# One-hot operations of an expert-gate scatter: per-token rows read from PSUM, two products in one operation

## The chip, the cores and the metric

One core of a Trainium2 chip runs the whole program. The metric is device time in microseconds (us), the median of several executions. One more execution is taken with the hardware profiler, and every row below is from it. Engines: PE is the matrix engine (PEld its weight loads), DVE the vector engine, ACT the scalar engine, POOL the GpSimd engine, and SP issues most DMAs. Each engine runs its own instructions in the order in which they were written, and semaphores make it wait for the others.

## The reference, cut to what matters

The program is one encoder block on 512 tokens of width 1024, in fp32: a convolution branch and windowed attention, both merged into x, and then PEER, a retrieval over 16384 experts that are one neuron each. The part around the change is PEER:

```python
q = (hc @ w_query).reshape(TOKEN_CHUNK, 8, 2, 128)
sc = einsum('thpd,pnd->thpn', q, sub_keys)          # 8 heads, 2 halves, 128 keys
vals, idx = top_k(sc, 16)
cand = vals[:, :, 0, :, None] + vals[:, :, 1, None, :]
top_s, pos = top_k(cand, 16)                        # 16 experts (i*128 + j) per head
gate = softmax(top_s)
act = gelu(einsum('thkd,td->thk', expert_u[expert_idx], hc))
out = einsum('thk,thkd->td', gate * act, expert_v[expert_idx])
```

So each token has 8 x 16 = 128 triples (i, j, gate).

## The kernel before, in words

Tokens are handled in four tiles of 128. For tile 0 the chosen rows of the expert tables are gathered. For tiles 1 to 3 (384 tokens) the whole tables are multiplied: with `hps`, PE computes U·h for each block of 128 experts (a "U block", `u_block`, 24 matmuls in split fp32: `uhi` from ACT, `ulo` from POOL, three products), ACT applies Gelu (`hb`), DVE multiplies by the dense gates (`hb<-hb,gt`), and PE accumulates the product with V in six PSUM tiles (`acc`, a "V block", 18 matmuls). The loop over 128 expert blocks at the end of the program, the V stage, does both. Thirty U blocks, the lead, are done ahead of it and kept in SBUF.

The dense gates G[token, i, j] are made by `build(t)`, once per tile t = 1, 2, 3, between the top-k and the V stage. It transposes i, j and gate to have the 128 triples on the partitions (L584, into `tp`), writes them as fp16 into `tt`, each number twice in a row, so that a row can be read in pairs (L591 by ACT; L592 by DVE; the gate, times 32768, as a high and a low half). Then, for each group of eight tokens (16 groups per tile, 48 in all):

- L607, DVE: `oij` = (0..127 == i) and (0..127 == j) for eight tokens, 2048 fp16 elements per partition;
- L609, DVE, twice: `ohl` = one-hot of j times the high, then the low half of the gate, 1024 elements each;
- L615 and L616, PE: for each token, `gp` = high part and low part times one-hot of i, 16 matmuls;
- L618, ACT: two copies of four tokens each from `gp` (PSUM) to `st`.

After every fourth group (`c`), a DMA on SP (L619) stores `st`, 2 MB, to `gates_dram`. The V stage reads it back as `gt` (L665), so the first V block waits for the last store.

`oij` and `ohl` have two buffers each. Of the eight PSUM banks the U blocks use two, `tp` one and `gp` five.

The order of instructions on an engine is not the order of this text. A scheduler takes the recorded operations, with its own estimate of each one's time, and sets an order per engine: lead U blocks, the top-k of tile 0 (`first_topk`, `select`) and the builds are interleaved by it. Only the loop of the V stage has POOL's order fixed by hand.

Of the kernel before, what the change touches and what calls it, by code (L numbers as in the profile page):

```python
# [7 lines left out]
F32 = mybir.dt.float32  # L8
F32R = mybir.dt.float32r
F16 = mybir.dt.float16  # L10
I32 = mybir.dt.int32
U32 = mybir.dt.uint32
AF = mybir.ActivationFunctionType
OP = mybir.AluOpType
# [3 lines left out]
P = 128  # L18
# [9 lines left out]
NKEY = 128  # L28
# [6 lines left out]
TB8 = 8  # L35
# [9 lines left out]
def encoder_block(ctx, tc, x, g1, w_in, taps, dwb, lng, lnb, w_pw, sink, w_o, w_out, g2, g2row,  # L45
                  w_query, keys, ut, u, v, gfin, out):
    nc = tc.nc
    ACT, DVE, POOL, PE, SP = nc.scalar, nc.vector, nc.gpsimd, nc.tensor, nc.sync
# [68 lines left out]
    with ExitStack() as fc:  # L117
# [15 lines left out]
        with ExitStack() as x0c:  # L133
# [6 lines left out]
            with tc.manual_schedule(engines=ordered):  # L140
                ACT.activation(warm, epst, AF.Sqrt)
                for t in range(NT):
                    a = x0.tile([P, D], F32, name="xt", bufs=NT)
# [32 lines left out]
        with ExitStack() as ac:  # L176
# [45 lines left out]
            for i in range(2):  # L222
                ps = proj(w_in[26 + i], hT)
                a = aw.tile([P, 4, 3 * P], F32, name="L", bufs=3).rearrange("p a b -> p (a b)")[:, :S]
# [176 lines left out]
        for j in range(KD):  # L401
            ps = proj(w_pw[j], acT, lo_engine=DVE)
            a = sg[0][:, j, :]
# [42 lines left out]
    with ExitStack() as rc:  # L446
# [27 lines left out]
        def lead(n):  # L474
            for _ in range(n):
                if nlead[0] < LEAD:
                    u_block(nlead[0])
                    nlead[0] += 1
# [40 lines left out]
        with qc:  # L519
# [44 lines left out]
            for h in range(HP):  # L564
                scs = []
                for p in range(2):
                    n = 2 * h + p
# [11 lines left out]
        psg = rc.enter_context(tc.tile_pool(name="psg", bufs=2, space=PSUM))  # L579

        def build(t):
            tp = psg.tile([P, 3, P], F32, name="tp", bufs=1)
            for s in range(3):
                PE.transpose(tp[:, s, :], ij[t][:, s].rearrange("p h k -> p (h k)"), ident)  # L584
            def twice(s):
                a = tp[:, s, :].rearrange("p (g t) -> p g t", t=TB8)
                return a[..., None].to_broadcast([P, P // TB8, TB8, 2])

            tt = gw.tile([P, P // TB8, 4, TB8, 2], F16, name="tt", bufs=2)
            for s in range(3):  # L590
                ACT.activation(tt[:, :, s], twice(s), AF.Copy, scale=1.0 if s < 2 else GSC)  # L591
            DVE.scalar_tensor_tensor(tt[:, :, 3], twice(2), GSC, tt[:, :, 2], op0=OP.mult, op1=OP.subtract)  # L592
            for c in range(P // GT):
                st = gw.tile([P, NKEY, GT], F32, name="st", bufs=2)
                for q8 in range(GT // TB8):
                    lead(0)
                    n = c * GT + q8 * TB8
                    oij, ohl = (gw.tile([P, 2, TB8, NKEY], F16, name=nm, bufs=2) for nm in ("oij", "ohl"))

                    def rows(s):  # L600
                        a = tt[:, n // TB8, s:s + 2].rearrange("p s t b -> p (s t) b")
                        return a[:, :, None, :].to_broadcast([P, 2 * TB8, NKEY // 2, 2])

                    def prs(a):
                        return a.rearrange("p s t (a b) -> p (s t) a b", b=2)

                    DVE.tensor_tensor(prs(oij), iota8, rows(0), op=OP.is_equal)  # L607
                    for s in range(2):
                        DVE.tensor_tensor(prs(ohl)[:, s * TB8:(s + 1) * TB8], prs(oij)[:, TB8:],  # L609
                                          rows(2)[:, s * TB8:(s + 1) * TB8], op=OP.mult)  # L610
                    for q4 in range(TB8 // 4):
                        gp = psg.tile([P, 4, NKEY], F32, name="gp", bufs=5)
                        for k in range(4):
                            m = q4 * 4 + k
                            PE.matmul(gp[:, k, :], ohl[:, 0, m, :], oij[:, 0, m, :], start=True, stop=False)  # L615
                            PE.matmul(gp[:, k, :], ohl[:, 1, m, :], oij[:, 0, m, :], start=False, stop=True)  # L616
                        o = q8 * TB8 + q4 * 4
                        ACT.activation(st[:, :, o:o + 4], gp.rearrange("p t i -> p i t"), AF.Copy, scale=1.0 / GSC)  # L618
                SP.dma_start(gdram[:, :, (t - 1) * (P // GT) + c].rearrange("g j i t -> j g i t"),  # L619
                             st.rearrange("p (g i) t -> p g i t", i=GI))  # L620

        for t in range(1, NT):
            build(t)
# [197 lines left out]
```

## Time and profile before

| what | us |
| --- | --- |
| median of 3 runs (lowest, highest) | 1814.74 (1811.3, 1815.37) |
| the profiled execution's own time | 1812.98 |
| its span | 1811.2 |
| PE busy in it | 1734.4 (96%) |
| DVE busy | 1432.8 (79%) |
| POOL busy | 961.4 (53%) |
| ACT busy | 770.8 (43%) |

The span runs from the first to the last instruction; 1.8 us of the execution's time lie outside it. A busy share is an average over stages: in most of the span PE is busy without a gap, and in the stage of the builds it is not. Matmul records overlap, since they are pipelined, so PE's pace is read from the distance of their starts and not from their durations.

### The profile page before, as it was taken

To read this page: it belongs to the slowest core of one execution; us is meant where nothing else is said; L and a number is where in the kernel's file an instruction comes from. 1 tells how busy PE (TensorE), PEld (TensorE's weight loads), DVE (VectorE), ACT (ScalarE), POOL (GpSimd) and SP (SyncE) were. 2 spreads that over 40 slices of the span, in tenths; PEclk is the share of its full clock that TensorE was granted. 3 is DMA by queue.
4 is the path that set the end of the run, shared out by engine and by line. 5 is a ranking of instruction groups with operands and counts; after the bars stand their busy time and mean duration, and the time that the engine had idled before them with its cause. 6 is when DMAs were issued, how large, how long until landed. Compare 5 with 4: busy or idle time off the path is not lost.

```text
span 1811.2 us, 25192 instructions
## 1 busy us (share of the span) xinstructions
PE 1734.4 (96%) x8873; PEld 1484.2 (82%) x8873; DVE 1432.8 (79%) x2545; ACT 770.8 (43%) x1374; POOL 961.4 (53%) x741
## 2 busy tenths in 40 slices
PE   6999999989999978888999999999999999999998
PEld 5778877658888877767899999999999999999876
DVE  4999856674536999999989987887787777878874
ACT  4233257883343335555443433333333333333243
POOL 4444421020134445445448888778777778778511
PEclk8999999999999989999999999999999999999999
DMA  4223210024243113777878988888888888898972
GB/s 142 87 92 100 98 59 24 24 82 152 81 148 100 56 59 124 233 214 227 290 257 321 333 309 328 311 318 312 313 317 304 323 317 315 295 332 287 343 259 93
DMA packets 148942, 379.42 MB, mean 209 GB/s; under 512 B 11520, under 2 KB 63760, under 8 KB 148816
## 3 DMA queue, kind: packets, MB, share of 16 engines
q1 hardware_dynamic: 110832, 241.20, 38.1%
q0 software_dynamic: 37120, 134.52, 20.8%
q10 hardware_dynamic: 864, 2.10, 0.3%
q8 instruction: 69, 1.13, 0.2%
q14 instruction: 57, 0.47, 0.1%
HBM read 346.84 MB, written 30.93 MB: 209 GB/s over the span
## 4 chain that ended last, share of the span: by engine, by line
PE 68%; DVE 15%; issue 2%; DMA 2%; ACT 1%; POOL 1%; SPq 0%; POOLq 0%; DVEq 0%; ACTq 0%
PE acc L64 8%; PE acc L63 8%; PE acc L65 8%; PE hps L65 7%; PE hps L64 7%; PE hps L63 7%; PE mm L63 5%; PE mm L65 5%; PE mm L64 4%; DVE ohl L609 4%; DVE oij L607 3%; DMA row<-in_v_dram,eidx 1%; PE s L63 1%; PE pt L290 1%; PE s L64 1%
## 5 line engine op out<-in xcount | busy, mean ns | idle before, releaser
L58 POOL TENSOR_TENSOR ulo<-uraw,uhi 128x512 fp32r<-128x512 f32 x256 | 406.1, 1595 | 290.6 <-ACT uhi L57 271.0
L63 PE MATMUL hps<-big,uhi 128*128 128x384 f32 x1024 | 349.3, 341 | 2.2 <-ACT hb L442 2.1
L65 PE MATMUL hps<-big,ulo 128*128 128x384 f32 x1024 | 349.4, 341 | 0.9 <-POOL ulo L58 0.9
L64 PE MATMUL hps<-big,uhi 128*128 128x384 f32 x1024 | 349.0, 341 | 0.0
L64 PE MATMUL acc<-vlo,ph 128*128 128x512 f32 x768 | 300.7, 392 | 1.6 <-DVE vlo L58 1.6
L65 PE MATMUL acc<-vhi,pl 128*128 128x512 f32 x768 | 299.6, 390 | 0.0
L63 PE MATMUL acc<-vhi,ph 128*128 128x512 f32 x768 | 299.1, 391 | 0.4 <-ACT vhi L57 0.4
L58 POOL TENSOR_TENSOR wlo<-wraw,whi 128x512 fp32r<-128x512 f32 x120 | 157.8, 1318 | 203.5 <-ACT whi L57 202.0
L57 ACT ACTIVATE uhi<-uraw 128x512 fp32r<-128x512 f32 x256 | 160.1, 631 | 233.6 <-PE hps L64 140.9
L643 DVE SCALAR_TENSOR_TENSOR row<-row,h2tok 128x1024 f32<-128x1024 f32 x128 | 189.5, 1487 | 66.4 <-DMA row<-in_u_dram,eidx 66.3
L654 DVE SCALAR_TENSOR_TENSOR yacc<-row,dots,yacc 128x1024 f32<-128x1024 f32 x127 | 177.2, 1396 | 69.7 <-DMA row<-in_v_dram,eidx 69.4
L58 DVE TENSOR_TENSOR vlo<-vraw,vhi 128x1024 fp32r<-128x1024 f32 x128 | 188.6, 1474 | 18.9 <-ACT vhi L57 18.9
L636 POOL DMA_INDIRECT row<-in_u_dram,eidx x128 | 183.8, 1436 | 33.2 <-issue 21.1
L63 PEld LDWEIGHTS hps<-big,uhi 128*128 128x128 f32 x1024 | 194.3, 190 | 6.6 <-ACT hb L442 2.5
L64 PEld LDWEIGHTS hps<-big,uhi 128*128 128x128 f32 x1024 | 194.6, 190 | 4.2
L57 ACT ACTIVATE whi<-wraw 128x512 fp32r<-128x512 f32 x152 | 95.3, 631 | 239.2 <-PE mm L64 125.5
L65 PEld LDWEIGHTS hps<-big,ulo 128*128 128x128 f32 x1024 | 194.2, 190 | 2.0 <-POOL ulo L58 1.9
L636 POOL DMA_INDIRECT row<-in_v_dram,eidx x128 | 165.1, 1290 | 48.7 <-DVE yacc L654 21.5
L57 ACT ACTIVATE ph<-hb 128x384 fp32r<-128x384 f32 x128 | 66.8, 523 | 287.4 <-PE acc L64 274.6
L65 PEld LDWEIGHTS acc<-vhi,pl 128*128 128x128 f32 x768 | 144.2, 188 | 30.9 <-DVE pl L58 0.3
L64 PEld LDWEIGHTS acc<-vlo,ph 128*128 128x128 f32 x768 | 144.2, 188 | 30.0 <-DVE vlo L58 3.7
L63 PEld LDWEIGHTS acc<-vhi,ph 128*128 128x128 f32 x768 | 144.1, 188 | 28.4 <-ACT vhi L57 1.0
(221 smaller groups left out, 3211.7 us busy)
## 6 DMA issues: line engine op xcount, KB each, us to landing
uraw<-in_ut_dram SPq DMA_DIRECT2D x128, 512.0 KB
vraw<-in_v_dram SPq DMA_DIRECT2D x128, 512.0 KB
gates_dram<-st SPq DMA_DIRECT2D x12, 2048.0 KB
gt<-gates_dram SPq DMA_DIRECT2D x32, 768.0 KB
wraw<-in_w_in_dram SPq DMA_DIRECT2D x44, 512.0 KB
wraw<-in_w_query_dram SPq DMA_DIRECT2D x16, 512.0 KB
wraw<-in_w_o_dram SPq DMA_DIRECT2D x8, 512.0 KB
oraw<-in_w_out_dram SPq DMA_DIRECT2D x16, 256.0 KB
```

The source lines that it names most:

```text
L57: ACT.activation(hi, src, AF.Copy)
L58: lo_engine.tensor_tensor(lo, src, f(hi), op=OP.subtract)
L63: PE.matmul(ps, wh, mh, start=first and i == 0, stop=False)
L64: PE.matmul(ps, wh, ml, start=False, stop=False)
L65: PE.matmul(ps, wl, mh, start=False, stop=last and i == n - 1)
L290: PE.transpose(pt[:, i, :], L[:, i, j * P:(j + 1) * P], ident)
L607: DVE.tensor_tensor(prs(oij), iota8, rows(0), op=OP.is_equal)
L609: DVE.tensor_tensor(prs(ohl)[:, s * TB8:(s + 1) * TB8], prs(oij)[:, TB8:], rows(2)[:, s * TB8:(s + 1) * TB8], op=OP.mult)
L636: POOL.indirect_dma_start(out=row, out_offset=None, in_=table, in_offset=bass.IndirectOffsetOnAxis(ap=eidx[:, c:c + 1], axis=0))
L643: DVE.scalar_tensor_tensor(row, row, 1.0, h2tok, op0=OP.mult, op1=OP.mult, accum_out=dots[:, c:c + 1])
L654: DVE.scalar_tensor_tensor(yacc, row, dots[:, c:c + 1], yacc, op0=OP.mult, op1=OP.add)
```

## The change

`tt`, the small table of rows, is copied once per tile by ACT into a PSUM tile `tq`, as 512 fp32 words that hold 1024 fp16 numbers. The one-hot operations read their rows from `tq`. The two products of a group become one operation on 2048 elements, whose other operand, the one-hot of j, is read twice by a stride of zero. The transposes now write a buffer of the `gp` ring, which has four banks instead of five; `tq` has the two that this and `tp` leave.

```diff
--- before.py
+++ after.py
@@ -579,7 +579,7 @@
         psg = rc.enter_context(tc.tile_pool(name="psg", bufs=2, space=PSUM))
 
         def build(t):
-            tp = psg.tile([P, 3, P], F32, name="tp", bufs=1)
+            tp = psg.tile([P, 4, P], F32, name="gp", bufs=4)
             for s in range(3):
                 PE.transpose(tp[:, s, :], ij[t][:, s].rearrange("p h k -> p (h k)"), ident)
             def twice(s):
@@ -590,6 +590,9 @@
             for s in range(3):
                 ACT.activation(tt[:, :, s], twice(s), AF.Copy, scale=1.0 if s < 2 else GSC)
             DVE.scalar_tensor_tensor(tt[:, :, 3], twice(2), GSC, tt[:, :, 2], op0=OP.mult, op1=OP.subtract)
+            tq = psg.tile([P, 512], F32, name="tq", bufs=2)
+            ACT.activation(tq, tt.rearrange("p g s t b -> p (g s t b)").bitcast(F32), AF.Copy)
+            tqv = tq.bitcast(F16).rearrange("p (g s t b) -> p g s t b", s=4, t=TB8, b=2)
             for c in range(P // GT):
                 st = gw.tile([P, NKEY, GT], F32, name="st", bufs=2)
                 for q8 in range(GT // TB8):
@@ -598,18 +601,19 @@
                     oij, ohl = (gw.tile([P, 2, TB8, NKEY], F16, name=nm, bufs=2) for nm in ("oij", "ohl"))
 
                     def rows(s):
-                        a = tt[:, n // TB8, s:s + 2].rearrange("p s t b -> p (s t) b")
+                        a = tqv[:, n // TB8, s:s + 2].rearrange("p s t b -> p (s t) b")
                         return a[:, :, None, :].to_broadcast([P, 2 * TB8, NKEY // 2, 2])
 
                     def prs(a):
                         return a.rearrange("p s t (a b) -> p (s t) a b", b=2)
 
                     DVE.tensor_tensor(prs(oij), iota8, rows(0), op=OP.is_equal)
-                    for s in range(2):
-                        DVE.tensor_tensor(prs(ohl)[:, s * TB8:(s + 1) * TB8], prs(oij)[:, TB8:],
-                                          rows(2)[:, s * TB8:(s + 1) * TB8], op=OP.mult)
+                    jj = oij[:, 1].rearrange("p t (a b) -> p t a b", b=2)
+                    DVE.tensor_tensor(ohl.rearrange("p s t (a b) -> p s t a b", b=2),
+                                      jj[:, None].to_broadcast([P, 2, TB8, NKEY // 2, 2]),
+                                      rows(2).rearrange("p (s t) a b -> p s t a b", s=2), op=OP.mult)
                     for q4 in range(TB8 // 4):
-                        gp = psg.tile([P, 4, NKEY], F32, name="gp", bufs=5)
+                        gp = psg.tile([P, 4, NKEY], F32, name="gp", bufs=4)
                         for k in range(4):
                             m = q4 * 4 + k
                             PE.matmul(gp[:, k, :], ohl[:, 0, m, :], oij[:, 0, m, :], start=True, stop=False)
```

The scheduler sets another order. The lines behind the change are numbered 3 or 4 higher: L607 is now L610, L609 is L612, L615 and L616 are L619 and L620.

On DVE, in the middle of the builds, one group and a half before (`vals`, `topv` and `topi` are the top-k of tile 0):

```order
L458 MAX topv_4514<-rep 128x8
L609 TENSOR_TENSOR ohl<-oij,tt 128x1024 x2
L607 TENSOR_TENSOR oij<-iotar,tt 128x2048
L459 MAX_INDEX topi_4518<-topv_4514,rep 128x8
L609 TENSOR_TENSOR ohl<-oij,tt 128x1024 x2
```

and with the change:

```order
L612 TENSOR_TENSOR ohl<-oij,tq 128x2048
L610 TENSOR_TENSOR oij<-iotar,tq 128x2048
L454 MAX topv_4514<-cand 128x8
L612 TENSOR_TENSOR ohl<-oij,tq 128x2048
L610 TENSOR_TENSOR oij<-iotar,tq 128x2048
```

Two products have become one of twice the size, and the one top-k instruction per group stays behind `oij`. From the first `oij` to the last `ohl`, 57 instructions of DVE that are neither stand before, and 96 with the change: more of tile 0's top-k lies inside the builds.

On PE, where a group's gate matmuls begin (`hps` are lead U blocks), before:

```order
L64 MATMUL hps<-big,uhi 128x384
L615 LDWEIGHTS ohl
L615 MATMUL gp<-oij,ohl 128x128
L615 LDWEIGHTS ohl
L615 MATMUL gp<-oij,ohl 128x128
L65 MATMUL hps<-big,ulo 128x384
L63 MATMUL hps<-big,uhi 128x384
L616 LDWEIGHTS ohl
L616 MATMUL gp<-oij,ohl 128x128
```

and with the change:

```order
L64 MATMUL hps<-big,uhi 128x384
L619 LDWEIGHTS ohl
L619 MATMUL gp<-oij,ohl 128x128
L620 LDWEIGHTS ohl
L620 MATMUL gp<-oij,ohl 128x128
```

A group's 16 gate matmuls stood in two pieces, two that need the high product alone and fourteen, with two or three `hps` between; they are one piece now, and nine `hps` (eight at times) stand between one group and the next. Counted over the order: 164 `hps` stand ahead of tile 1's transposes in both. From there to the first gate matmul it was 74 and is 86, to the last one 500 and now 592. Between the last gate matmul and the first `acc` of the V stage there were 121 and are 60.

On PE, the transposes of tile 2 before:

```order
L63 MATMUL hps<-big,uhi 128x384
L584 MATMUL tp<-ident,ij_4512 128x128 x3
L64 MATMUL hps<-big,uhi 128x384
```

and with the change:

```order
L620 LDWEIGHTS ohl
L620 MATMUL gp<-oij,ohl 128x128
L584 MATMUL gp<-ident,ij_4512 128x128 x3
L64 MATMUL hps<-big,uhi 128x384
```

They stood ahead of tile 1's first group and stand behind its last one now; those of tile 3 stand likewise behind tile 2's last group.

## Rows read from the trace of the kernel before

**Rows 1.** Windows, two stretches: us, then busy per engine (count), PE clock, DMA share, GB/s

```profile
686.00:855.00 169.00, 139.30 (x1227) 117.41 (x1227) 168.95 (x255) 86.58 (x165) 79.23 (x47) 0.98 0.65 199
...
1000.00:1400.00 400.00, 400.00 (x2026) 364.71 (x2025) 333.39 (x387) 150.93 (x242) 325.25 (x223) 1.00 0.86 316
```

**Rows 2.** Waits, 686 to 855 us: who for whom, us, times, longest

```profile
PEld L615 <- DVE ohl L609: 36.1, 40, 2.6
```

**Rows 3.** Lines by shape, 685 to 855 us

```profile
L609 DVE TENSOR_TENSOR ohl<-oij,tt 128x1024 f16<-128x1024 f16 x96 | 83.6, 912 | 0.0
L58 POOL TENSOR_TENSOR ulo<-uraw,uhi 128x512 fp32r<-128x512 f32 x38 | 72.8, 1916 | 75.5 <-ACT uhi L57 57.8 <-PE hps L65 17.7
L607 DVE TENSOR_TENSOR oij<-iotar,tt 128x2048 f16<-128x2048 f16 x48 | 69.7, 1457 | 0.0
...
L57 ACT ACTIVATE uhi<-uraw 128x512 fp32r<-128x512 f32 x39 | 24.7, 634 | 22.0 <-PE hps L64 15.0 <-issue 6.0 <-POOL ulo L58 0.5
```

**Rows 4.** Tile tt: ns min/median/max, first and last start

```profile
L609 DVE TENSOR_TENSOR ohl<-oij,tt x96: 665/680/1769, 691.8 to 850.4; 128x1024 f16<-128x1024 f16 x96
L607 DVE TENSOR_TENSOR oij<-iotar,tt x48: 1209/1214/2320, 687.6 to 847.6; 128x2048 f16<-128x2048 f16 x48
```

**Rows 5.** Timeline, 730 to 748 us: start, duration

```profile
737.24 0.22 PE L615 MATMUL gp<-oij,ohl 128*128 128x128 f16 x1
...
737.91 0.22 PE L616 MATMUL gp<-oij,ohl 128*128 128x128 f16 x1
...
738.26 3.27 DVE L609 TENSOR_TENSOR ohl<-oij,tt 128x1024 f16<-128x1024 f16 x2
738.38 0.34 PE L64 MATMUL hps<-big,uhi 128*128 128x384 f32 x1
...
738.56 0.34 PE L65 MATMUL hps<-big,ulo 128*128 128x384 f32 x1
...
739.51 1.47 POOL L58 TENSOR_TENSOR ulo<-uraw,uhi 128x512 fp32r<-128x512 f32 x1 [0.21 <-ACT uhi L57]
```

**Rows 6.** Tile olo, the row of DVE

```profile
L58 DVE TENSOR_TENSOR olo<-oraw,ohi x8: 682/688/1778, 481.2 to 490.0; 128x512 fp32r<-128x512 f32 x8
```

**Rows 7.** Line 209, the convolution's step

```profile
L209 DVE SCALAR_TENSOR_TENSOR ca<-ub,tapt,ca x232: 735/752/756, 37.0 to 233.7; 128x512 f32<-128x512 f32 x116
```

**Rows 8.** Lines of POOL, 90 to 180 us

```profile
L58 POOL TENSOR_TENSOR wlo<-wraw,whi 128x512 fp32r<-128x512 f32 x32 | 41.6, 1301 | 47.6 <-ACT whi L57 47.6
```

**Rows 9.** Lines of DVE by shape, whole span

```profile
L405 DVE TENSOR_TENSOR sg<-sg,sg 128x512 f32<-128x512 f32 x8 | 5.5, 689 | 0.1
L393 DVE TENSOR_TENSOR x<-mm,x 128x512 f32<-128x512 f32 x8 | 5.5, 688 | 15.0 <-PE mm L65 15.0
```

**Rows 10.** Tile oh

```profile
L501 DVE TENSOR_TENSOR oh<-iota,fd x8: 1201/1214/2331, 602.8 to 914.1; 128x2048 f16<-128x2048 f16 x8
...
L508 DVE TENSOR_REDUCE ij<-oh x8: 2260/2270/2272, 605.5 to 920.6; 128x128 f32<-128x2048 f16 x8
```

**Rows 11.** Tile gp, the row of line 616

```profile
L616 PE MATMUL gp<-oij,ohl x384: 219/219/330, 693.4 to 853.0; 128*128 128x128 f16 x192
```

**Rows 12.** Timeline of SP's DMA issues, 684 to 900 us

```profile
854.31 0.74 SPq L619 DMA_DIRECT2D gates_dram<-st  x1
856.65 5.79 SPq L431 DMA_DIRECT2D uraw<-in_ut_dram  x2
...
864.04 0.42 SPq L665 DMA_DIRECT2D gt<-gates_dram  x1
```

**Rows 13.** Chain that ended last, 600 to 900 us

```profile
875.20 1.67 PE acc L63 x6
```

**Rows 14.** Timeline of PE, 655 to 676 us

```profile
672.66 0.66 PE L584 MATMUL tp<-ident,ij 128*128 128x128 f32 x2 [7.19 <-DVE ij L508]
```

**Rows 15.** Windows, as Rows 1, around that wait

```profile
672.00:676.00 4.00, 2.97 (x10) 2.60 (x11) 4.00 (x21) 0.77 (x2) 1.62 (x3) 0.50 0.41 135
676.00:680.00 4.00, 4.00 (x20) 4.00 (x19) 4.00 (x12) 2.41 (x4) 2.12 (x2) 0.79 0.36 133
```

## The prediction

> **What bounds the kernel now.** I read the windows first, to find the stretch where PE isn't saturated. From 1000 to 1400 us PE is busy throughout [rows 1], so the V stage is PE's, and the end moves only if PE's idle time moves. In the stage of the builds, 686 to 855 us, PE is busy 139.3 of 169 us and DVE 168.95 [rows 1]: DVE sets the pace there. The waits say for what: PE's weight loads waited 36.1 us for `ohl`, in 40 waits [rows 2]. The groups by line give DVE's load: `ohl` 83.6 us and `oij` 69.7 us, 153.3 together [rows 3], and 168.95 - 153.3 = 15.7 us are top-k work.
>
> Then the spread. `oij` takes 1209 ns at least, 1214 in the median and 1457 in the mean; `ohl` 665, 680 and 912 [rows 3, 4]. So most run at the floor, and some are 1.1 us longer. The timeline shows such a case: two products take 3.27 us where twice the median is 1.36, and a subtraction of POOL, `ulo`, runs inside them [rows 5]. POOL pays as well: `ulo` takes 1916 ns in this stage [rows 3], while the same subtraction took 1301 beside the convolution [rows 8]. What differs is where DVE's second operand lies. The convolution's step reads one operand in SBUF and one in PSUM, and its 232 instances lie between 735 and 756 ns, with POOL at work beside them [rows 7, 8]. `olo` reads both from SBUF, and takes from 682 to 1778 ns [rows 6]. I take the stretch to be a collision of DVE's second SBUF operand with POOL, which an operand in PSUM avoids.
>
> **The change part by part.** I carry the last gate matmul, 853.0 us now [rows 11], and then the first `acc`, 875.2 us [rows 13], to the new program.
>
> One-hot operations: 48 `oij` and 48 `ohl` of 2048 elements replace 144 operations. Neither reads two operands from SBUF any more. Does a PSUM operand cost time? With 512 fp32 elements the addition with one operand in PSUM (L393) took 688 ns and the one with both in SBUF (L405) took 689 [rows 9]: nothing. Whether 2-byte elements from PSUM still go two at a time, no row shows. The ends are 1.21 us, a 2048-element fp16 operation of two operands at its quiet median, and 2.27 us, the reduction that reads the same 2048 elements one at a time [rows 10]. I take 1.21, since the pairs lie in PSUM as they do in `tt`, side by side, and rows 9 show the source to be neutral; 96 x 1.21 = 116.2 us, that is 37.1 us less. The lower end can't be much lower, as no such operation ran under 1.20 us [rows 10].
>
> The Trainium skill speaks against this step. Its page VectorE: DVE Perf Modes, section The perf-mode tier table, gives a two-tensor operation with any PSUM operand one element per cycle; the same page's Why PSUM operands drop a tier caps it at two, and at one for fp32 only. The trace has no 16-bit PSUM operand to decide between the two sentences. By the first, the time is that of rival A; by the second, that of the forecast. The page's table of cycles (The TRN2 errata section) also gives 120 instead of 58 fixed cycles for a PSUM source; by it, 96 operations would cost 96 x 62 / 0.96 GHz = 6 us more, an estimate from that page. The 688 against 689 ns of rows 9 do not bear it out.
>
> Top-k inside the builds: 96 instead of 57 small DVE instructions. At 15.7 / 57 = 0.275 us, that is +10.7 us in this stage (and as much less later, where DVE is not the limit).
>
> The copy to `tq`: three ACT copies of 128x512, 0.63 us each by `uhi` [rows 3]; ACT is busy 86.6 of 169 us [rows 1], which hides them. They lengthen the way from the transposes to the first `oij`. The transposes of tiles 2 and 3 now stand behind the last gate matmul of the tile before, so the whole chain (transposes, ACT's copies, DVE's, `tq`) lies open at those two places, except for the 15 and 19 top-k instructions which DVE has there, 4 to 5 us. I charge 1 us at each, 0 to 3 being possible: +2.
>
> DVE's stage: -37.1 + 10.7 + 2 = -24.4 us, and the last gate matmul at 853.0 - 24.4 = 828.6.
>
> PE in the same stage: is it late next? From the first gate matmul, near 692.5, when the first `ohl`, started at 691.8 [rows 4], is done, it has 592 - 86 = 506 `hps` and 768 gate matmuls. Starts of `hps` are 0.175 apart (0.18 in rows 5), those of gate matmuls 0.056 (twelve steps from 737.24 to 737.91) [rows 5]: 88.6 + 43.0, and some 5 for 96 changes between the kinds, an estimate. 692.5 + 137 = 829.5. So both engines would need the same time. With two buffers between them they will not mesh fully; I add 0.15 us per group, 7 us in all, a choice. Last gate matmul: 836.
>
> The way to the V stage is late next. Now it takes 22.2 us from the last gate matmul to the first `acc`: the last store is issued at 854.31, the read of `gt` that needs it at 864.04 [rows 12], and DVE has 61 top-k instructions between its last `ohl` and its first `hb<-hb,gt` in either order, some 61 x 0.275 = 17 us. The 121 `hps` that stood there cover 121 x 0.175 = 21.2 us, and PE loses nothing. Sixty now cover 10.5. Two lead loads stand between that store and that read, and take 5.79 us until POOL frees their buffers [rows 12]; with half as many lead blocks left, POOL should free them earlier. I take 20 us for the chain, between 17 and 22; so PE idles 9.5 us and the first `acc` starts at 856. The only such pause in the builds cost more than itself: after 7.19 us idle [rows 14] the clock stood at 0.50 and, in the next four microseconds, at 0.79 on average [rows 15], 2 us lost. I charge 2 again.
>
> In exchange, 31 more `hps` are done by then (816 against 785 by the order), 5.4 us.
>
> Sum: 856 - 875.2 = -19.2; -5.4; +2: -22.6 us. The profiled execution's 1812.98 becomes 1790.4; the median is 1.76 above that execution, so 1792.
>
> **The rivals.** *A, 2-byte elements from PSUM go one at a time.* For it: no row shows a 2-byte PSUM operand at the paired rate. Against: rows 9, for fp32. DVE then needs 96 x 2.27 + 26.4 + 2 = 246 us for the stage, 77 more than now; last gate matmul at 930, first `acc` at 950, 5.4 regained and 2 lost: 71 us more, 1886. It decides for slower as soon as an operation takes over 1.52 us: 96 x 1.52 - 153.3 + 12.7 (top-k and copies) - 2.2 (shorter chain) - 5.4 + 2 is about zero.
>
> *B, the stretch has another cause and stays.* For it: POOL's own work is the same in kind. Against: rows 6 and 7. Then 96 x 1.457 + 26.4 + 2 = 168 us, as now; the last gate matmul at 852, the first `acc` at 872, less 5.4, plus 2: 1806 for the profiled execution, 1808 for the median. The change would then do little of what it says.
>
> *C, the engines mesh and the end is shorter.* Last gate matmul at 829, 17 us to the first `acc` (DVE's top-k alone): 846, less 5.4, plus 2, that is 32 us less: 1783. Against it: two engines with equal loads and two buffers between them.
>
> **How the numbers follow.** Forecast, 1784 to 1802 (the 7 us of meshing between 0 and 14, the pause between 6 and 13): 0.57. C and anything better: 0.09. B, or most of the gain lost to meshing, 1802 to 1815: 0.16, of which 0.05 lie within 0.2% (3.6 us) of the median, about what a measurement of this kernel can tell from no change. A, or a part of it: 0.18. That gives faster 0.77, same 0.05, slower 0.18. The range leaves out A and the far ends: 1778 to 1812. The likeliest case's own range is 1784 to 1802.
>
> **What would show it.** `oij` and `ohl` in the new profile at 1.21 us each, with a narrow spread: right on the pair mode and the collision; 2.2 us means A; a median of 1.21 with a mean near 1.46 means B. `ulo` falling from 1916 towards 1301 ns would confirm the collision from POOL's side. The last gate matmul should be near 836, and a pause of PE of some 9 us should stand before the first `acc`, with the clock at 0.50 behind it. If that pause is missing, or if the V stage from there to the end takes longer than now for as many matmuls, my last steps are wrong.

## The result, and the profile after

The changed kernel takes 1787.49 us in the median of four runs (1785.7 to 1793.01), the kernel before, in runs beside it, 1813.28 (1811.3 to 1815.37): the ratio is 0.9859, 95% interval [0.9843, 0.9876], 25.8 us less. Predicted were 1792 us, and 22.6 us less; the time lies in the range that was called likeliest, 1784 to 1802. The profiled execution took 1785.7 us, with a span of 1783.8.

The windows of the changed kernel, in the columns of [rows 1]: the builds, the way to the V stage, and the middle of that stage.

```profile
686.00:830.00 144.00, 142.55 (x1310) 134.56 (x1309) 142.76 (x265) 95.59 (x182) 62.51 (x58) 1.00 0.80 247
830.00:860.00 30.00, 18.00 (x94) 15.97 (x92) 27.61 (x94) 12.31 (x21) 9.15 (x11) 0.77 0.92 320
...
1000.00:1400.00 400.00, 400.00 (x2026) 364.78 (x2025) 334.14 (x376) 150.81 (x243) 327.76 (x222) 1.00 0.86 315
```

In the builds PE and DVE are now both busy, 142.55 and 142.76 of 144 us, where PE had 139.3 of 169 [rows 1]. The V stage is as it was. The new hole lies between: PE is busy 18 of 30 us.

Tile `tq`: minimum, median and maximum in ns, first and last start.

```profile
L610 DVE TENSOR_TENSOR oij<-iotar,tq x48: 1203/1209/1216, 690.5 to 826.5; 128x2048 f16<-128x2048 f16 x48
L612 DVE TENSOR_TENSOR ohl<-oij,tq x48: 1182/1200/1212, 693.3 to 827.9; 128x2048 f16<-128x2048 f16 x48
L594 ACT ACTIVATE tq<-tt x3: 602/602/603, 688.9 to 787.1; 128x512 f32<-128x512 f32 x3
```

The floor of [rows 4] has become the whole distribution: the largest `oij` is 1216 ns where it was 2320. With 58.1 and 57.6 us for the two, DVE's one-hot work is 115.7 us where it was 153.3 [rows 3]. POOL's side, from the groups of 685 to 830 us, which answers to the `ulo` of [rows 3] at 1916 ns:

```profile
L58 POOL TENSOR_TENSOR ulo<-uraw,uhi 128x512 fp32r<-128x512 f32 x47 | 60.6, 1293 | 74.3 <-ACT uhi L57 72.1 <-ACT st L622 2.3
```

The waits of 686 to 850 us, in the columns of [rows 2]; there PE's weight loads had waited 36.1 us for `ohl`:

```profile
PEld L619 <- issue: 5.2, 33, 0.2
...
PEld L619 <- DVE ohl L612: 4.1, 14, 1.7
```

The gate matmuls (tile `gp`; the last one before is in [rows 11]), the first line from the kernel before and two from the changed one, and the first `acc` (timeline of PE; before in [rows 13]):

```profile
L615 PE MATMUL gp<-oij,ohl x384: 219/219/330, 692.5 to 852.9; 128*128 128x128 f16 x192
...
L619 PE MATMUL gp<-oij,ohl x384: 219/219/232, 694.6 to 830.6; 128*128 128x128 f16 x192
L620 PE MATMUL gp<-oij,ohl x384: 219/219/219, 694.7 to 830.6; 128*128 128x128 f16 x192
```

```profile
853.34 1.65 PE L63 MATMUL acc<-vhi,ph 128*128 128x512 f32 x3 [12.00 <-ACT vhi L57]
```

So the last gate matmul comes at 830.6 where it came at 853.0, the first `acc` at 853.3 where it came at 875.2, and PE stood still for 12.00 us in between. From the first gate matmul to the last it is 136.0 us where it was 160.5; in this execution the stage began 2.1 us later. The windows around that pause show the clock, the third number from the right:

```profile
840.00:844.00 4.00, 1.34 (x8) 1.02 (x6) 3.86 (x18) 1.29 (x3) 1.72 (x3) 1.00 0.83 274
844.00:848.00 4.00, 0.00 (x0) 0.00 (x0) 3.97 (x6) 0.00 (x0) 1.18 (x1) 0.59 0.96 349
848.00:852.00 4.00, 0.00 (x0) 0.00 (x0) 4.00 (x8) 1.12 (x3) 0.00 (x0) 0.50 1.04 428
852.00:856.00 4.00, 2.66 (x6) 1.78 (x7) 3.26 (x6) 3.97 (x6) 0.00 (x0) 0.50 0.41 138
856.00:860.00 4.00, 4.00 (x14) 3.17 (x13) 3.57 (x6) 0.84 (x4) 0.00 (x0) 0.70 0.92 345
```

The clock falls to its lower level during the pause and stays there for some microseconds of work: 2.7 us at 0.50 and 4 at 0.70 are 2.5 us lost, by this count. What PE waits for is in the chain that ended last (start, us, what), and in SP's timeline:

```profile
844.10 2.17 DVE oh L501
...
847.62 2.23 DVE ij L508
850.29 0.57 DVE hb L678
850.88 1.46 ACT ph L57 x3
852.34 0.96 ACT vhi L57
853.34 1.65 PE acc L63 x3
```

```profile
831.56 0.38 SPq L623 DMA_DIRECT2D gates_dram<-st  x1
...
835.35 5.17 SPq L431 DMA_DIRECT2D uraw<-in_ut_dram  x2
...
841.52 0.42 SPq L669 DMA_DIRECT2D gt<-gates_dram  x1
```

DVE works off tile 0's top-k until 850, one instruction behind the other, and only then gates the first U block. One of these instructions, `oh` with both operands in SBUF, takes 2.17 us there where its median is 1.21, so the collision is still met in the top-k. But the gates come hardly sooner. From issue to landing, the last store and the first read of `gt` took (line L623 at 831.56, tile `gt` at 841.52):

```profile
DMA to landing us min/median/max: 8.9/8.9/8.9
...
DMA to landing us min/median/max: 7.9/7.9/7.9
```

So the store landed at 840.4 and the gates at 849.4, 0.9 us before DVE turned to them at 850.3. Two chains of nearly equal length end here; which of them would hold the first `acc` by itself is seen in the variants below.

### The profile page after: what moved, and what is told of

Same layout as the page of the kernel before. It is cut to its first block, busy times and chain, and to the rows that moved or that the text cites. A ratio compares the mean times of both kernels' runs of the same rounds, so it can differ in the third digit from the quotient of the medians.

```text
span 1783.8 us, 25146 instructions
## 1 busy us (share of the span) xinstructions
PE 1725.8 (97%) x8873; PEld 1490.2 (84%) x8873; DVE 1387.3 (78%) x2497; ACT 772.8 (43%) x1377; POOL 935.5 (52%) x741
## 4 chain that ended last, share of the span: by engine, by line
PE 78%; DVE 8%; ACT 2%; DMA 1%; issue 0%; SPq 0%; POOL 0%; ACTq 0%; DVEq 0%
PE hps L65 9%; PE hps L64 9%; PE hps L63 9%; PE acc L64 9%; PE acc L63 9%; PE acc L65 9%; PE mm L65 5%; PE mm L63 5%; PE mm L64 5%; PE gp L619 1%; PE s L63 1%; PE gp L620 1%; DMA vraw<-in_v_dram 1%; PE pt L290 1%; PE s L64 1%; PE s L65 1%
## 5 line engine op out<-in xcount | busy, mean ns | idle before, releaser
L58 POOL TENSOR_TENSOR ulo<-uraw,uhi 128x512 fp32r<-128x512 f32 x256 | 383.2, 1502 | 307.6 <-ACT uhi L57 303.3
L57 ACT ACTIVATE uhi<-uraw 128x512 fp32r<-128x512 f32 x256 | 160.5, 632 | 236.4 <-PE hps L64 154.4
L647 DVE SCALAR_TENSOR_TENSOR row<-row,h2tok 128x1024 f32<-128x1024 f32 x128 | 184.8, 1449 | 71.7 <-DMA row<-in_u_dram,eidx 71.3
L58 DVE TENSOR_TENSOR vlo<-vraw,vhi 128x1024 fp32r<-128x1024 f32 x128 | 193.2, 1509 | 18.0 <-ACT vhi L57 17.9
```

What stands on the lines that cost most here:

```text
L57: ACT.activation(hi, src, AF.Copy)
L58: lo_engine.tensor_tensor(lo, src, f(hi), op=OP.subtract)
L647: DVE.scalar_tensor_tensor(row, row, 1.0, h2tok, op0=OP.mult, op1=OP.mult, accum_out=dots[:, c:c + 1])
```

## The experiments

Each was timed beside the kernel before (medians there 1813.5 to 1814.8 us). Two questions: is the gain the collision, the merging or the order; and is the pause worth anything?

**Merging alone.** The two products in one, rows from `tt`:

```diff
-            tq = psg.tile([P, 512], F32, name="tq", bufs=2)
-            ACT.activation(tq, tt....bitcast(F32), AF.Copy)
...
-                        a = tqv[:, n // TB8, s:s + 2]...
+                        a = tt[:, n // TB8, s:s + 2]...
```

> The two products in one operation, but all rows still read from SBUF (no tq). Collision theory (DVE's second SBUF operand collides with POOL): oij stays at a mean near 1.45 us with cases above 2.2, the merged ohl has a mean of 1.4 to 1.6 us with cases above 2.2, ulo stays near 1.9 us; merging saves 48 operations' fixed cost of some 0.1 us, 5 us at most, and the time is 1805 to 1813. Rival (fewer operations and the new order give the gain, PSUM nothing): 1787 to 1793.

Measured: 1816.65 us, ratio 1.001 [1.000, 1.002]. Tile `oij` of that run:

```profile
L607 DVE TENSOR_TENSOR oij<-iotar,tt x48: 1186/1212/2292, 690.2 to 857.7; 128x2048 f16<-128x2048 f16 x48
L609 DVE TENSOR_TENSOR ohl<-oij,tt x48: 1197/1214/2314, 693.9 to 860.0; 128x2048 f16<-128x2048 f16 x48
```

The tails are back, the means are 1414 and 1641 ns, `ulo` is at 1847. DVE's one-hot work is 145.4 us, 7.9 less than before; the order puts 88 instead of 57 other instructions inside the builds, which at the prediction's 0.275 us eats 8.5. So merging alone gives nothing here; the counts say that what it saves, the order spends. The mean of `ohl` lies just above the expected 1.4 to 1.6 us, and the time 4 us above the expected range.

**PSUM alone.** Rows from `tq`, two products as before:

```diff
-                    jj = oij[:, 1].rearrange("p t (a b) -> p t a b", b=2)
-                    DVE.tensor_tensor(ohl..., jj..., rows(2)..., op=OP.mult)
+                    for s in range(2):
+                        DVE.tensor_tensor(prs(ohl)[:, s * TB8:(s + 1) * TB8], prs(oij)[:, TB8:],
+                                          rows(2)[:, s * TB8:(s + 1) * TB8], op=OP.mult)
```

> Rows from PSUM, but two products of 1024 elements as before. Collision theory: oij 1.21 us and ohl 0.67 us, both with a spread under 0.05 us, ulo near 1.3 us; DVE has 48 x (2 x 0.67 - 1.20) = 6.7 us more than in the changed kernel; the order leaves only 38 hps for the pause before the first acc but has done 25 more before it: 1788 to 1796. Rival (merging gives the gain): 1805 or more.

Measured: 1798.85 us, ratio 0.9916 [0.9899, 0.9932], tile `oij` and PE's timeline:

```profile
L612 DVE TENSOR_TENSOR ohl<-oij,tq x96: 651/674/682, 692.9 to 839.2; 128x1024 f16<-128x1024 f16 x96
L610 DVE TENSOR_TENSOR oij<-iotar,tq x48: 1199/1212/1223, 689.3 to 837.2; 128x2048 f16<-128x2048 f16 x48
```

```profile
864.10 1.65 PE L63 MATMUL acc<-vhi,ph 128*128 128x512 f32 x3 [15.37 <-ACT vhi L57]
```

The durations are as expected. The time is 3 us over what I wrote: the last gate matmul comes at 841.8, 11 us later than in the changed kernel, where PE has 25 more `hps` to do in the stage (4.4 us) and DVE 3.4 us more of one-hot work (119.1 against 115.7); PE's weight loads wait 8.8 us for `ohl` there, against 4.1. What else delays it I did not trace. With 38 `hps` as cover, PE's pause is 15.37 us.

**The other operand in PSUM.** In `oij` the 0..127 row lies in PSUM and the index rows are read from `tt`:

```diff
+        ACT.activation(iop[:, :NKEY // 2], iotar.bitcast(F32), AF.Copy)
...
-                    DVE.tensor_tensor(prs(oij), iota8, rows(0), op=OP.is_equal)
+                    DVE.tensor_tensor(prs(oij), iotap, rows(0), op=OP.is_equal)
```

> In oij the other operand comes from PSUM: the 0..127 row lies there, and the index rows are read from SBUF (tt) as before; ohl as in the changed kernel. So each operation has one SBUF operand. Collision theory: oij again at 1.21 us with a narrow spread, time 1785 to 1795. Rival (it is the row that is read again and again from SBUF that is slow): oij as before, mean near 1.45, maximum near 2.3, 8 to 12 us lost against the changed kernel.

Measured: 1784.42 us, ratio 0.984 [0.9823, 0.9856].

```profile
L614 DVE TENSOR_TENSOR oij<-iop,tt x48: 1185/1210/1225, 687.4 to 818.8; 128x2048 f16<-128x2048 f16 x48
L616 DVE TENSOR_TENSOR ohl<-oij,tq x48: 1194/1206/1216, 690.6 to 821.0; 128x2048 f16<-128x2048 f16 x48
```

The same index rows of `tt`, read over and over from SBUF, are not slow when the other operand is in PSUM. What counts is that only one operand is in SBUF. This settles the cause against the rival.

That the other party is POOL can be read from the trace of the kernel before, operation by operation. The longest `oij` and the POOL instruction that was running when it began (timelines of DVE and of POOL):

```profile
709.68 2.32 DVE L607 TENSOR_TENSOR oij<-iotar,tt 128x2048 f16<-128x2048 f16 x1
...
707.55 3.37 POOL L58 TENSOR_TENSOR ulo<-uraw,uhi 128x512 fp32r<-128x512 f32 x1 [5.34 <-PE hps L65]
```

POOL's instruction had 1.23 us left, and the operation took 1.11 us more than the median. So it is with all of them: of the 144 one-hot operations there, 40 are longer than the usual 1.21 and 0.67 us, by 0.08 to 1.11 us. Each of them began while a POOL instruction ran, and is longer by what that one had left, less about 0.12 us. Together that is 34.5 us. The 89 that began with POOL idle lie within 0.02 us of the usual time. The other 15 began beside a POOL instruction with 1.3 us or more left, and are not stretched. In the changed kernel 43 of the 96 operations began while POOL ran, and none is stretched.

**Rival A's price.** The rows in PSUM are read with a last step of zero:

```diff
-                        return a[:, :, None, :].to_broadcast([P, 2 * TB8, NKEY // 2, 2])
+                        return a[:, :, None, 0:1].to_broadcast([P, 2 * TB8, NKEY // 2, 2])
```

> The changed kernel, but the last step over the rows in PSUM is zero: the first of the two equal numbers is read for each element, so elements don't lie in pairs. This prices rival A of the prediction (one element at a time). Expected: oij and ohl at 2.2 to 2.3 us, DVE needs some 100 us more for the builds and PE idles; the order puts all lead blocks into the builds and none into the way to the V stage: 1880 to 1900. If PSUM operands went two at a time whatever the steps: 1787.

Measured: 1887.42 us, ratio 1.040 [1.0383, 1.0417].

```profile
L610 DVE TENSOR_TENSOR oij<-iotar,tq x48: 2272/2277/2289, 691.8 to 931.5; 128x2048 f16<-128x2048 f16 x48
L612 DVE TENSOR_TENSOR ohl<-oij,tq x48: 2249/2270/2283, 695.7 to 933.9; 128x2048 f16<-128x2048 f16 x48
```

Without pairs an operation takes 2.27 us, the upper end that the reduction of [rows 10] gave, and the whole comes within 2 us of the 1886 worked out for rival A. That it is so close is in part luck: the last gate matmul comes at 937.8, where that sum had 930. The pairs are worth 100 us here.

**The pause.** It has a cause in the order: ahead of the first `acc` the changed kernel has 816 `hps`, 34 U blocks, which is as many as fit, 32 in the ring of `hb` and two in PSUM. So the scheduler had nothing left to put there. Two more buffers, with the convolution's taps in a pool that is closed early to make room:

```diff
-    hring = ctx.enter_context(tc.tile_pool(name="hring", bufs=LEAD + 2))
+    hring = ctx.enter_context(tc.tile_pool(name="hring", bufs=LEAD + 4))
...
-            tapt = const.tile([P, KD, TAPS], F32, name="tapt")
+            tapt = gat.tile([P, KD, TAPS], F32, name="tapt")
```

> The changed kernel as it is, for a time beside its variants. Expected: 1787 us, ratio to the kernel before 0.986; PE pauses about 12 us before the first acc, with the last gate matmul near 830 and the first acc near 853 us.

Measured: 1788.11 us, ratio 0.9861 [0.9845, 0.9878], with 11.98 us of pause.

> The changed kernel with 34 instead of 32 buffers for the finished U blocks (hb); to make room the convolution's taps lie in a pool that is closed early. In the order 108 hps instead of 60 now stand between the last gate matmul and the first acc. Theory (PE's pause before the first acc is lost time, and it is there because the ring of U blocks is full): the 48 extra hps take 8.4 us of the 12 us pause, the first acc stays near 853 us, and the time falls by 7 to 10 us, to about 1779. Rival (the start of the V stage is bound elsewhere, by DVE's or POOL's share or the gathers, so that work done earlier there is waited for later): the same time as the changed kernel, 1787, within 2 us.

Measured: 1781.84 us, ratio 0.9825 [0.9808, 0.9841]; PE's timeline before the first `acc`:

```profile
850.84 0.45 PE L63 MATMUL hps<-big,uhi 128*128 128x384 f32 x1 [0.83 <-ACT hb L442]
858.38 1.67 PE L63 MATMUL acc<-vhi,ph 128*128 128x512 f32 x6 [2.95 <-ACT vhi L57]
```

The pause is 0.83 + 2.95 = 3.8 us, and the clock stays at full speed behind it:

```profile
855.00:860.00 5.00, 2.05 (x10) 1.45 (x9) 4.98 (x10) 4.08 (x8) 0.23 (x1) 1.00 0.63 254
```

Of the 8.2 us of pause, 6.3 show in the time; the rival, which had 1787, is out. The first `acc` comes at 858.4 and not near 853 as expected, and the time is 3 us over the 1779 that I wrote. The gate matmuls ran from 696.6 to 835.1 there, and from 693.4 to 829.4 in the run of the changed kernel beside it; why they began 3 us later, with the same order ahead of them, I have not found out. In the two traces with the order of the kernel before, they begin at 692.5 and, with 34 buffers, at 697.0.

> The changed kernel with 34 buffers for the U blocks, on the same chip: 1782 us again, ratio to the kernel before 0.983.

Measured: 1783.7 us (1781.05 to 1785.87), ratio 0.9833 [0.9819, 0.9847], 3.65 us of pause.

> The kernel before with 34 buffers for the U blocks: its order has 121 hps at that place with 32 buffers and with 34. Theory: no pause there, nothing to win, ratio 1.000 within 0.002. If more buffers help by themselves, as by freer POOL and ACT, it is faster by some us.

Measured: 1814.67 us, ratio 1.0003 [0.9993, 1.0012]. The order is that of the kernel before on every engine. Here the buffers help only where a pause is.

> As the run with 34 buffers, with 36, and three instead of four buffers for the gated U blocks (ph, pl) to pay for them. The order has 118 hps in the pause. Theory: 10.2 us of the pause are covered, 1777 us. If three ph buffers hold PE up in the V stage, the time is longer than with 34 buffers; the rival says 1787.

Measured: 1784.01 us (1780.62 to 1787.39), ratio 0.9843 [0.9822, 0.9864]. The pause is down to 1.9 us, but the time is no better than with 34 buffers, and 7 us over the 1777 expected. Three `ph` buffers seem to cost something: in the V stage, from 860 us on, PE waits for the gated blocks, where with 34 buffers and four `ph` it waited 0.3 to 1.2 us in all:

```profile
PE acc L65 <- DVE pl L58: 5.2, 6, 1.5
```

> The kernel with the 0..127 row in PSUM and the index rows in SBUF, with 34 buffers for the U blocks: its order has 118 hps before the first acc, 106 with 32 buffers. If what sets these kernels apart is only PE's pause before the first acc (4.4 us with 32 buffers here, 12 us in the changed kernel, 3.8 us in the changed kernel with 34), then 2 us of pause go, and the time is 1780 to 1784, level with the changed kernel with 34 buffers. If the place of the operands matters by itself, it is 3 us or more away from that one.

Measured: 1780.86 us (1778.89 to 1784.46), ratio 0.9819 [0.9804, 0.9835]; PE's timeline:

```profile
848.73 1.85 PE L63 MATMUL acc<-vhi,ph 128*128 128x512 f32 x6 [2.25 <-ACT vhi L57]
```

It is the fastest version measured, 33 us under the kernel before and some 7 under the changed one, but its interval overlaps that of the changed kernel with 34 buffers. The place of the operands is not shown to set them apart. The pauses and the times together:

| kernel | `hps` as cover | pause, us | median, us |
| --- | --- | --- | --- |
| PSUM, two products | 38 | 15.4 | 1798.9 |
| changed | 60 | 12.0 | 1787.5, 1788.1 |
| 0..127 row in PSUM | 106 | 4.4 | 1784.4 |
| changed, 34 buffers | 108 | 3.8, 3.7 | 1781.8, 1783.7 |
| changed, 36 buffers | 118 | 1.9 | 1784.0 |
| 0..127 row in PSUM, 34 buffers | 118 | 2.3 | 1780.9 |

**What holds the first `acc`.** In some of these runs the order leaves a part of the top-k until after the first gated U block, so that DVE is free early. DVE's first `hb` with merging alone, with the 0..127 row in PSUM, and with that and 34 buffers:

```profile
881.13 1.49 DVE L675 TENSOR_TENSOR hb<-hb,gt 128x384 f32<-128x384 f32 x3 [8.40 <-DMA gt<-gates_dram]
...
843.28 1.50 DVE L682 TENSOR_TENSOR hb<-hb,gt 128x384 f32<-128x384 f32 x3 [6.93 <-DMA gt<-gates_dram]
...
845.83 1.49 DVE L682 TENSOR_TENSOR hb<-hb,gt 128x384 f32<-128x384 f32 x3 [7.05 <-DMA gt<-gates_dram]
```

DVE stands idle 7 to 8 us until the gates land, and from the last gate matmul to the first `acc` it is still 21.3, 23.0 and 23.0 us. So without the top-k in it this way is no shorter: the store of the gates and their way back hold it as well. With PSUM and two products DVE stands idle 9.8 us there, which the profile puts down to a load of V, and the way is 22.3 us.

## Why the prediction was right

- *One-hot operations at 1.21 us.* 1.210 and 1.200 in the mean, 115.7 us for the 116.2 predicted. The Trainium skill's page VectorE: DVE Perf Modes has two sentences on this. The one under Why PSUM operands drop a tier is borne out for 16-bit pairs: 2048 elements took 1.209 us in the median, and 2.27 us with the last step at zero. The 1x that The perf-mode tier table gives for any PSUM operand is not borne out by these 1.209 us. Nor are the 6 us estimated from the fixed cycles of that Trainium skill page (The TRN2 errata section): it is 1.209 us with an operand from PSUM in the median, and 1.214 with both from SBUF.
- *The collision.* Shown by the operands: with one in SBUF no operation is stretched, whichever it is; with two in SBUF the tails return, whether merged or not. And it is POOL: the stretches equal what was left of its instruction. Rival B is out. POOL gained its part, 1916 to 1293 ns.
- *Top-k inside the builds, the open chains at tiles 2 and 3 (+10.7, +2).* DVE's sum gave 24.4 us less for the stage. From the first to the last gate matmul it is 24.4 us less, 136.0 for 160.5.
- *PE's need in the stage.* 137 us were counted, and the stage took 136.0. That DVE and PE would need the same time was right.
- *Meshing, 7 us.* This term was mis-sized: PE waited 4.1 us for `ohl` in all, and the last gate matmul came at 830.6, near the sum without that term (829.5). Two buffers were enough here, where each group brings the same work to both engines.
- *The way to the V stage, 20 us.* It is 22.7, no shorter than before (22.2), so the pause was 12.0 instead of 9.5 us. Here the mechanism was wrong too: the prediction had DVE's top-k (17 us) as the floor of this way, and let POOL shorten it by freeing the last lead buffers earlier. SP still waited 5.17 us for them, where it was 5.79 [rows 12]; and without the top-k, the store, the read behind it and the steps from there to the first `acc` would have taken all but 0.9 us of the 22.7. Rival C was right that the engines mesh, and wrong in the 17 us of the top-k alone.
- *The clock, 2 us.* 2.5 by the windows. What of it reaches the end is seen in PE's time from the first `acc` to the last, before and after:

```profile
875.20:1803.00 927.80, 926.19 (x4590) 831.27 (x4591) 747.98 (x846) 354.65 (x562) 652.61 (x456) 1.00 0.82 299
...
853.30:1775.70 922.40, 922.03 (x4559) 827.59 (x4560) 727.52 (x779) 350.04 (x554) 645.51 (x446) 1.00 0.83 299
```

PE is busy 4.2 us less, where the 31 `hps` done ahead are worth 5.4; so about 1.2 us of the clock's cost can be seen here, and 2.8 in the other pair of traces (925.6 us with 34 buffers before, 923.0 in the repeat of the changed kernel). The V stage did not get longer otherwise. In the first pair PE also idles 1.2 us less.

With the measured terms the sum is 853.3 - 875.2 = -21.9, less 4.2 and 1.2 from there to the last `acc`: -27.3 us, which is what the two profiled executions differ by. The medians differ by 25.8; the changed kernel's runs lie up to 7.3 us apart, and the profiled one is the fastest of them. The forecast came within 5 us of both because its errors have opposite signs: 7 us too much for meshing, 2.7 too little for the way to the V stage. The first was a choice, and that the second offset a part of it was luck.

## What to carry to other kernels

Look at the spread of an operation, not only at its mean: behind a tight floor with a tail there was another engine in the way here. The operations that do not have the tail tell by which operand, and what runs when a long one begins tells which engine. When the stage with idle time gets faster, follow its end to the next stage: what had covered the hand-over (here 121 matmuls, then 60) may have been used up, and a few more buffers can buy it back. The last thing on a chain is not all that holds it: another chain can end a microsecond before, and a variant that moves the first away shows it. A scheduler with its own costs moves other work into whatever you shorten, so a part of a change, tried by itself, can give its saving away to the order.

## What the runs showed of the hardware

- A collision of a two-operand DVE instruction in SBUF with a POOL subtraction costs DVE up to 1.1 us, namely what is left of POOL's instruction less 0.12 us, and POOL about 0.6 us in the mean (1916 for 1293 ns); one operand of DVE's in PSUM takes it away for both.
- A 2048-element fp16 operation with one operand in PSUM takes 1.21 us when its elements lie in pairs and 2.27 us when the last step is zero.
- After 12 us of idle PE the clock stood at 0.50 and was back at 1.00 in the window from 860 us; a pause of 2.95 us left it at 1.00.
- The 2 MB store of the last gates landed 8.9 us after its issue, and the first read behind it 7.9 us after its own.
